# Sharing out the norm's last steps otherwise, and the next input's affine on ScalarE alone

## The chip, the cores and the metric

The kernel runs on one core of one Trainium2 chip. The metric is the device time of one execution in microseconds; less is better. The profile is of one execution by the hardware profiler, with its own time.

## The reference, cut to what matters

A two-layer network on 256 context and 512 latent tokens of width 1024. Each layer has an FFN, a mixer (a gated recurrence with pooling in layer 0, differential attention in layer 1) and a second FFN; a layer norm follows each of them, and the next sub-step's input is the norm's output scaled and shifted, with other factors for context and for latent tokens.

```python
def modulate(x, shift, scale):
    return x * (1.0 + scale) + shift

def ffn_substep(x, mods, w_in, w_out, g, b):
    shift, scale, gate = mods
    y = swiglu(modulate(x, shift, scale), w_in, w_out)
    return layer_norm(ALPHA * x + MACARON * gate * y, g, b)
...
x = ffn_substep(x, m_lat[0:3], ...)
ctx = ffn_substep(ctx, m_ctx[0:3], ...)
h_lat = modulate(x, m_lat[3], m_lat[4])
h_ctx = modulate(ctx, m_ctx[3], m_ctx[4])
```

## The kernel before, in words

**Layout.** Features lie on the 128 partitions, in KB = 8 blocks of 128; tokens lie along the row, context (0 to 256) first, then latent (256 to 768). Products are made in three passes for accuracy: each operand is split into a rounded high part and a remainder. `split` (lines 117 to 119) casts the high part on ScalarE and subtracts on VectorE (or GpSimd) for the low part. `mm3` (lines 157 to 159) issues high x high, high x low and low x high.

**An output product** is `out_phase`. It has two passes over the same weights, for two spans of tokens, the halves: for three FFNs and the even mixer tokens 0 to 512 and 512 to 768 (`FULL`), for the odd mixer and the last FFN 256 to 512 and 512 to 768 (`LATS`). A pass has nh steps kk, each over 256 rows of the weights: 11 for an FFN, 4 for a mixer. A step is two groups q of 24 matmuls. `operands` splits a step's g tile and its two weight tiles; in an FFN's second pass the weights' high and low parts go to tiles named `spare`, of which there are 11, shared with the first half's data. `fetch` starts the loads two steps ahead on SyncE's queue, into the four buffers of `raw`.

**The norm of the first half** runs during the second pass. `layer_norm` is a generator with 22 yields: four for sums, one for the mean, eight for the deviations and their squares, one for the variance and its inverse root rs, and eight final steps j, one for each feature block. After each step of the second pass `out_phase` takes three of them (-(-25 // 11) for an FFN) or seven (for a mixer). A final step j multiplies `r` by rs on VectorE (line 329), makes the next input `h` from it segment by segment (the first segment on ScalarE, line 336, the second on GpSimd, line 338), splits `h` into `xh` and `xl` (ScalarE, VectorE), makes the residual in place in `r` on GpSimd (line 344), and writes that to `ax` in memory on SyncE's queue (line 348). In the last FFN there is no next input: the final step makes the output in place, on ScalarE or GpSimd by turns, and writes it. The norm of the second half has only latent tokens; it goes on under the next sub-step's first products.

**Order.** The framework's planner fixes each engine's instruction order when the kernel is built, from readiness in a timing model of its own and, among ready ones, from the order in the program; buffers limit how far it runs ahead. On the chip each engine goes through its queue in order.

Of the kernel before, what the change touches and what calls it, by code (L numbers as in the profile page):

```python
# [15 lines left out]
AF = mybir.ActivationFunctionType  # L16
ALU = mybir.AluOpType
# [25 lines left out]
class Net:  # L43
# [255 lines left out]
    def layer_norm(self, half, halves, aff, nxt, ax_new, r_of, s1, done, table):  # L299
        nc = self.nc  # L300
        c0, c1 = halves[half]
        n = c1 - c0
        for j in range(done, KB):
            self.add_up(s1, r_of(half, j), j)
            if j % 2:
                yield
        pm = self.mean(s1, n, half)
        s2 = self.sums(n)
        yield
        for j in range(KB):  # L310
            r = r_of(half, j)
            nc.vector.tensor_sub(out=r, in0=r, in1=pm)
            sq = s2[j] if j < 2 else self.tmp("sq")[:, :n]
            i = nc.scalar.activation(out=sq, in_=r, func=AF.Square)
            if j == 0 and not half:
                self.table(LOGEXP, i)
            if j > 1:
                self.add_up(s2, sq, j)
            yield
        pv = self.mean(s2, n, half)  # L320
        rs, rt = self.tmp("rs"), self.tmp("rt")
        i = self.rsqrt(pv, self.eps_ln, LN_EPS, rs[:, :n], rt[:, :n])
        if half and table:
            self.settled = i
            self.table(table, i)
        yield
        for j in range(KB):
            r = r_of(half, j)
            nc.vector.tensor_mul(out=r, in0=r, in1=rs[:, :n])
            if nxt is not None:  # L330
                h = self.tmp("h")
                for x, (v, a, b) in enumerate(self.segs(c0, c1)):
                    o, i, sc, sh = h[:, a - c0:b - c0], r[:, a - c0:b - c0], aff[:, 2 + 2 * v, j:j + 1], \
                        aff[:, 3 + 2 * v, j:j + 1]
                    if x == 0:
                        nc.scalar.activation(out=o, in_=i, func=AF.Identity, scale=sc, bias=sh)
                    else:
                        nc.gpsimd.tensor_scalar(out=o, in0=i, scalar1=sc, scalar2=sh, op0=ALU.mult, op1=ALU.add)
                self.split(self.xh[:, j, c0:c1], self.xl[:, j, c0:c1], h[:, :n])
            g, b = aff[:, 0, j:j + 1], aff[:, 1, j:j + 1]  # L340
            if nxt is None and j % 2:
                nc.scalar.activation(out=r, in_=r, func=AF.Identity, scale=g, bias=b)
            else:
                nc.gpsimd.tensor_scalar(out=r, in0=r, scalar1=g, scalar2=b, op0=ALU.mult, op1=ALU.add)
            if nxt is None:
                nc.sync.dma_start(out=self.out[:, j, c0 - NCTX:c1 - NCTX], in_=r)
            else:
                nc.sync.dma_start(out=ax_new[:, j, c0:c1], in_=r)
            yield
# [18 lines left out]
    def out_phase(self, pool, nk, wsrc, gload, halves, gate, l, i, nxt, r_of, table=None, keep=False, ada=iter(())):  # L368


        nc = self.nc
        aff = self.affine(l, i, nxt)
# [4 lines left out]
        nh = nk // 2  # L377
        steps = [(p, kk) for p in range(2) for kk in range(nh)]

        kept, loaded, held = {}, {}, []  # L380

        def fetch(step):

            half, kk = step
            if half:
                loaded[step] = [gload(kk, *halves[half])]
                if not keep:
                    loaded[step] += [self.raw() for q in range(2)]
                for q, r in enumerate(loaded[step][1:]):
                    nc.sync.dma_start(out=r, in_=wsrc(q, kk))  # L390

        def operands(step):
            half, kk = step
            g, *raw = loaded.pop(step, (None,))
            g = self.pair2(gload(kk, *halves[half]) if g is None else g, halves[half][1] - halves[half][0])
            if raw:
                ws = []
                for r in raw:
                    ws.append([self.spare(pool, F32R) for _ in range(2)])
                    self.split(*ws[-1], r)  # L400
                return g, ws
            if not half:
                ws = [self.weights(wsrc(q, kk), "vector", pool if keep and kk else None) for q in range(2)]
                if not keep:
                    return g, ws
                kept[kk] = ws
            return g, kept[kk]
# [3 lines left out]
        for n_step, (half, kk) in enumerate(steps):  # L411
            c0, c1 = halves[half]
            n = c1 - c0
            if kk == 0:
                if n > 256:
                    out = [self.ps("st" if f == KB - 1 else "h")[:, :n] for f in range(KB)]
                else:
                    two = [self.ps() for f in range(KB // 2)]
                    out = [two[f // 2][:, f % 2 * n:f % 2 * n + n] for f in range(KB)]

            def products(kk, ops, q):
                (gh, gl), ws = ops
                wh, wl = ws[q]
                for k2 in range(2):
                    for f in range(4):
                        w0 = k2 * 512 + f * P
                        self.mm3(out[4 * q + f], wh[:, w0:w0 + P], wl[:, w0:w0 + P], gh[:, k2, :], gl[:, k2, :],
                                 kk + k2 == 0 and (n > 256 or f % 2 == 0),
                                 2 * kk + k2 == nk - 1 and (n > 256 or f % 2 == 1))

            if nxt is None and half and kk >= nh - 2:
                held.append((kk, ops))
                if kk == nh - 1:
                    for _ in norm:
                        pass
                    self.finale(held, products, out, gate, aff, [r_of(1, j) for j in range(KB)], halves[1])
                    break
            else:
                for q in range(2):
                    products(kk, ops, q)  # L440
            if n_step + 1 < len(steps):
                ops = operands(steps[n_step + 1])
            if n_step + 2 < len(steps):
                fetch(steps[n_step + 2])
            if half == 0:
                with self.behind_weights():
                    next(ada, None)
            if kk == 1:
                if half:
                    self.RB = self.late().rearrange("p (k c) -> p k c", k=KB)  # L450
                for j in range(KB):
                    self.residual(r_of(half, j), j, c0, c1)
            if half:
                for _ in range(-(-25 // nh)):
                    next(norm, None)
            if kk < nh - 1:
                continue
            if half:
                for _ in norm:
                    pass  # L460
            s1 = self.sums(n)
            for j in range(KB):
                r = r_of(half, j)
                for (v, a, b) in self.segs(c0, c1):
                    nc.vector.scalar_tensor_tensor(
                        out=r[:, a - c0:b - c0], in0=out[j][:, a - c0:b - c0],
                        scalar=self.col(*gate, v, j), in1=r[:, a - c0:b - c0], op0=ALU.mult, op1=ALU.add)
                if half:
                    self.add_up(s1, r, j)
            norm = self.layer_norm(half, halves, aff, nxt, ax_new, r_of, s1, KB if half else 0, table)  # L470
# [989 lines left out]
```

## Time and profile before

| | us |
|---|---|
| median of 3 runs | 2761.28 |
| lowest, highest | 2757.34, 2761.32 |
| the profiled execution's own time | 2760.27 |
| its span, first to last instruction | 2758.1 |

The mean granted TensorE clock of the profiled execution is 0.99 of full speed. PE is TensorE, PEld its weight loads, DVE VectorE, ACT ScalarE, POOL GpSimd, SP SyncE; a q behind the name is the engine's queue of DMA issues. L119 is line 119 of the kernel before. In the views an instruction is named by what it writes and reads, as `xh<-h`, with partitions x elements. What an engine waited for stands behind its idle time as `<-` and the engine, tile and line that ended it. A full clock is 1.00, half of it 0.50.

### The profile page before, as it was taken

The numbers are of one execution on the slowest core, as the hardware profiler recorded it, in microseconds if no ns is written. First come the engines' busy times: TensorE is split into PE (matmuls) and PEld (weight loads), VectorE is DVE, ScalarE is ACT, GpSimd is POOL, SyncE is SP. The second block draws the span as 40 slices with busy tenths as digits, with TensorE's granted clock in tenths as the row PEclk, the third lists the DMA queues.
The fourth block names the chain that finished last, engine by engine and source line by source line (L and its number), as shares of the span: only waits on it lengthen the run. The fifth ranks groups of instructions, "written<-read, shape, count | busy, mean of one in ns | idle before, by whom it ended". The sixth has DMA issues, their size and how long they took to land. (4 is left out here: it accounts for less than half of the span.)

```text
span 2758.1 us, 43943 instructions
## 1 busy us (share of the span) xinstructions
PE 2667.8 (97%) x17386; PEld 2435.0 (88%) x17386; DVE 1966.3 (71%) x2922; ACT 1221.4 (44%) x1922; POOL 888.1 (32%) x680
## 2 busy tenths in 40 slices
PE   8999999999989999999999999999999998999998
PEld 6999988987778789999888999988887777999997
DVE  4899677847764789977786776556827786787666
ACT  3433433634442533433254444423534655555554
POOL 2545300422110554440055444201422211465302
PEclk9999999999999999999999999999999999999999
DMA  6443266521104334426663432265521112433563
GB/s 250 138 155 129 88 244 231 202 78 68 45 22 168 111 131 143 140 91 221 217 201 117 172 123 78 94 230 197 199 77 47 35 39 79 140 100 116 171 212 129
DMA packets 138770, 374.20 MB, mean 136 GB/s; under 512 B 16066, under 2 KB 47170, under 8 KB 138564
## 3 DMA queue, kind: packets, MB, share of 16 engines
q1 hardware_dynamic: 136256, 369.68, 38.6%
q8 instruction: 136, 2.23, 0.3%
q10 hardware_dynamic: 2308, 1.72, 0.2%
q14 instruction: 70, 0.57, 0.1%
HBM read 337.78 MB, written 33.56 MB: 135 GB/s over the span
## 5 line engine op out<-in xcount | busy, mean ns | idle before, releaser
L117 ACT CAST r4h<-raw 128x1024 fp32r<-128x1024 f32 (+1 forms) x322 | 332.8, 1035 | 625.7 <-PE ps L158 325.0
L157 PE MATMUL ps<-xh,r4h 128*128 128x512 f32 (+2 forms) x1732 | 583.7, 339 | 11.4 <-ACT xh L117 7.6
L158 PE MATMUL ps<-xl,r4h 128*128 128x512 f32 (+2 forms) x1732 | 580.8, 336 | 0.5 <-DVE xl L119 0.4
L159 PE MATMUL ps<-xh,r4l 128*128 128x512 f32 (+2 forms) x1732 | 580.4, 336 | 0.4 <-DVE r4l L119 0.4
L119 DVE TENSOR_TENSOR r4l<-raw,r4h 128x1024 fp32r<-128x1024 f32 (+1 forms) x306 | 373.2, 1221 | 223.5 <-ACT r4h L117 163.6
L157 PEld LDWEIGHTS ps<-xh,r4h 128*128 128x128 f32 x1732 | 326.5, 189 | 41.3 <-ACT xh L117 10.1
L158 PEld LDWEIGHTS ps<-xl,r4h 128*128 128x128 f32 x1732 | 327.4, 189 | 22.9 <-DVE xl L119 2.0
L159 PEld LDWEIGHTS ps<-xh,r4l 128*128 128x128 f32 x1732 | 327.8, 189 | 22.2 <-DVE r4l L119 0.9
L157 PE MATMUL ps<-six,r4h 128*128 128x384 f32 (+1 forms) x852 | 278.3, 327 | 6.0 <-ACT c L788 6.0
L157 PE MATMUL ps<-r4h 128*128 128x512 f32 (+1 forms) x768 | 276.4, 360 | 1.1 <-DVE g L903 1.1
L159 PE MATMUL ps<-r4h,r4l 128*128 128x512 f32 (+1 forms) x768 | 275.3, 359 | 0.7 <-DVE r4l L119 0.7
L158 PE MATMUL ps<-six,r4h 128*128 128x384 f32 (+1 forms) x852 | 275.9, 324 | 0.0
L159 PE MATMUL ps<-six,r4l 128*128 128x384 f32 (+1 forms) x852 | 275.4, 323 | 0.0
L158 PE MATMUL ps<-r4l,r4h 128*128 128x512 f32 (+1 forms) x768 | 275.3, 359 | 0.0
L159 PE MATMUL ps<-r4h,spare 128*128 128x256 f32 (+1 forms) x896 | 262.4, 293 | 9.8 <-DVE spare L119 9.8
L157 PE MATMUL ps<-r4h,spare 128*128 128x256 f32 (+1 forms) x896 | 266.0, 297 | 4.0 <-ACT spare L117 4.0
L158 PE MATMUL ps<-r4l,spare 128*128 128x256 f32 (+1 forms) x896 | 261.4, 292 | 0.0
L760 POOL TENSOR_TENSOR raw<-raw,late 128x512 f32<-128x512 f32 x71 | 93.6, 1319 | 400.4 <-DVE r4l L119 388.5
L119 DVE TENSOR_TENSOR r4l<-late,r4h 128x1024 fp32r<-128x1024 f32 x71 | 106.1, 1495 | 115.1 <-PE ps L158 97.2
L159 PEld LDWEIGHTS ps<-r4h,spare 128*128 128x128 f32 x896 | 174.8, 195 | 13.2 <-DVE spare L119 11.3
L157 PEld LDWEIGHTS ps<-r4h,spare 128*128 128x128 f32 x896 | 175.0, 195 | 8.6 <-ACT spare L117 4.6
L185 DVE SCALAR_TENSOR_TENSOR trash<-spare 128x1024 bf16<-128x1024 f32 x112 | 181.1, 1618 | 1.0 <-DMA spare<-in_w_ada 0.9
(313 smaller groups left out, 5646.6 us busy)
## 6 DMA issues: line engine op xcount, KB each, us to landing
raw<-in_w_ffn_in SPq DMA_DIRECT2D x176, 512.0 KB, 3.5
raw<-in_w_ffn_out SPq DMA_DIRECT2D x176, 512.0 KB, 4.3
spare<-in_w_ada SPq DMA_DIRECT2D x80, 512.0 KB, 5.3
six<-in_w_ada SPq DMA_DIRECT2D x64, 512.0 KB, 5.7
g<-late_g SPq DMA_DIRECT2D x88, 128.0 KB, 2.1
six<-g SPq DMA_DIRECT2D x44, 256.0 KB, 3.7
raw<-in_w_in_even SPq DMA_DIRECT2D x20, 512.0 KB, 3.5
raw<-in_w_in_odd SPq DMA_DIRECT2D x16, 512.0 KB, 3.4
```

The costliest lines, as they stand in the source:

```text
L117: self.copied = self.nc.scalar.copy(out=h, in_=src)
L119: eng.tensor_sub(out=l, in0=src, in1=h.bitcast(F32))
L157: mm(out=ps, lhsT=h, rhs=xh, start=first, stop=False)
L158: mm(out=ps, lhsT=h, rhs=xl, start=False, stop=False)
L159: mm(out=ps, lhsT=l, rhs=xh, start=False, stop=last)
L185: nc.vector.scalar_tensor_tensor(out=self.tmp("trash").bitcast(BF16), in0=r, scalar=1.0, in1=self.c_bc[v], op0=ALU.mult, op1=ALU.mult, acc ...
L760: nc.gpsimd.tensor_sub(out=a12, in0=a12, in1=sums[:, 512:])
```

## The change

It does two things. In a final step, all segments of `h` are made on ScalarE, where the second was on GpSimd. And where nh is 11, the steps of the norm that follow kk = 0 to 10 are given by a list, 3, 3, 3, 3, 3, 2, 2, 2, 2, 1, 1, where it was three after each; elsewhere the number stays. The computation is the same.

```diff
             if nxt is not None:
                 h = self.tmp("h")
-                for x, (v, a, b) in enumerate(self.segs(c0, c1)):
-                    o, i, sc, sh = h[:, a - c0:b - c0], r[:, a - c0:b - c0], aff[:, 2 + 2 * v, j:j + 1], \
-                        aff[:, 3 + 2 * v, j:j + 1]
-                    if x == 0:
-                        nc.scalar.activation(out=o, in_=i, func=AF.Identity, scale=sc, bias=sh)
-                    else:
-                        nc.gpsimd.tensor_scalar(out=o, in0=i, scalar1=sc, scalar2=sh, op0=ALU.mult, op1=ALU.add)
+                for v, a, b in self.segs(c0, c1):
+                    nc.scalar.activation(out=h[:, a - c0:b - c0], in_=r[:, a - c0:b - c0], func=AF.Identity,
+                                         scale=aff[:, 2 + 2 * v, j:j + 1], bias=aff[:, 3 + 2 * v, j:j + 1])
                 self.split(self.xh[:, j, c0:c1], self.xl[:, j, c0:c1], h[:, :n])
...
         kept, loaded, held = {}, {}, []
+
+
+        steps_of = (3, 3, 3, 3, 3, 2, 2, 2, 2, 1, 1) if nh == 11 else [-(-25 // nh)] * nh
...
             if half:
-                for _ in range(-(-25 // nh)):
+                for _ in range(steps_of[kk]):
                     next(norm, None)
```

## Rows read from the trace of the kernel before

**Rows 1.** The page's first part: busy time, share and instructions of each engine.

```profile
PE 2667.8 (97%) x17386; PEld 2435.0 (88%) x17386; DVE 1966.3 (71%) x2922; ACT 1221.4 (44%) x1922; POOL 888.1 (32%) x680
```

**Rows 2.** TensorE's waits over the whole run: total us, times, longest.

```profile
PE ps L159 <- DVE spare L119: 9.8, 7, 1.9
...
PE ps L157 <- ACT spare L117: 4.0, 3, 1.3
```

**Rows 3.** TensorE's timeline, first FFN's output product: start, duration, idle before.

```profile
532.11 0.39 PE L159 MATMUL ps<-r4h,spare 128*128 128x256 f32 x1 [1.16 <-DVE spare L119]
532.34 0.28 PE L157 MATMUL ps<-r4h,spare 128*128 128x256 f32 x1
532.46 0.28 PE L158 MATMUL ps<-r4l,spare 128*128 128x256 f32 x1
...
536.34 0.39 PE L157 MATMUL ps<-r4h,spare 128*128 128x256 f32 x1 [1.33 <-ACT spare L117]
...
538.79 0.58 PE L159 MATMUL ps<-r4h,spare 128*128 128x256 f32 x1 [1.94 <-DVE spare L119]
...
540.02 0.41 PE L158 MATMUL ps<-r4l,spare 128*128 128x256 f32 x1
540.24 0.42 PE L159 MATMUL ps<-r4h,spare 128*128 128x256 f32 x1
```

**Rows 4.** Stages: length, busy us (instructions) by engine, PEclk, DMA share, GB/s.

```profile
518.00:546.00 28.00, 23.57 (x172) 22.96 (x172) 22.02 (x27) 15.97 (x24) 21.66 (x16) 0.88 0.50 174
536.00:546.00 10.00, 7.71 (x42) 7.51 (x43) 9.05 (x10) 5.83 (x8) 5.50 (x3) 0.66 0.73 249
1444.00:1454.00 10.00, 8.06 (x45) 7.85 (x45) 8.58 (x9) 5.29 (x8) 4.88 (x3) 0.66 0.79 263
1972.00:1982.00 10.00, 7.77 (x51) 7.56 (x52) 9.05 (x10) 5.85 (x8) 5.46 (x3) 0.83 0.77 253
922.00:928.00 6.00, 5.14 (x16) 3.78 (x15) 4.34 (x6) 2.79 (x6) 6.00 (x7) 0.72 0.25 96
```

The engines stand in the order PE, PEld, DVE, ACT, POOL.

**Rows 5.** ScalarE's timeline in the same stage as rows 3.

```profile
527.37 1.04 ACT L117 CAST spare<-raw 128x1024 fp32r<-128x1024 f32 x1
529.34 0.60 ACT L336 ACTIVATE h<-spare,aff 128x256 f32<-128x256 f32 x1 [0.93 <-DVE spare L329]
532.36 0.62 ACT L117 CAST xh<-h 128x512 fp32r<-128x512 f32 x1 [2.41 <-POOL h L338]
532.88 1.09 ACT L336 ACTIVATE h<-spare,aff 128x256 f32<-128x256 f32 x2
...
535.25 1.99 ACT L117 CAST spare<-raw 128x1024 fp32r<-128x1024 f32 x2
```

**Rows 6.** Groups by line from 518 to 546: busy us, mean ns | idle before, releaser.

```profile
L119 DVE TENSOR_TENSOR xl<-h,xh 128x512 fp32r<-128x512 f32 x8 | 6.3, 805 | 5.9 <-ACT xh L117 5.9
...
L117 ACT CAST xh<-h 128x512 fp32r<-128x512 f32 x8 | 4.8, 620 | 8.3 <-POOL h L338 8.3
...
L119 DVE TENSOR_TENSOR r4l<-six,r4h 128x512 fp32r<-128x512 f32 x2 | 1.4, 679 | 0.0
```

**Rows 7.** Line 338 (GpSimd's affine), whole run: ns minimum/median/maximum, first and last start.

```profile
L338 POOL TENSOR_SCALAR h<-six,aff x12: 548/1260/2035, 519.7 to 1962.2; 128x256 f32<-128x256 f32 x12
L338 POOL TENSOR_SCALAR h<-spare,aff x12: 551/1768/3088, 529.8 to 1973.6; 128x256 f32<-128x256 f32 x12
L338 POOL TENSOR_SCALAR h<-R,aff x8: 547/767/2022, 918.1 to 934.0; 128x256 f32<-128x256 f32 x8
```

**Rows 8.** VectorE's timeline in the last FFN's output product.

```profile
2718.28 1.23 DVE L119 TENSOR_TENSOR spare<-raw,spare 128x1024 fp32r<-128x1024 f32 x1 [0.64 <-DMA out<-spare]
...
2733.89 1.66 DVE L485 SCALAR_TENSOR_TENSOR late<-ps,mod,late 128x256 f32<-128x256 f32 x4 [6.76 <-PE ps L159]
```

**Rows 9.** TensorE's waits from 878 to 962, the even mixer's output and after it.

```profile
PE ps L157 <- ACT xh L117: 3.5, 3, 1.6
```

**Rows 10.** VectorE's timeline after the even mixer's output product.

```profile
933.37 1.26 DVE L465 SCALAR_TENSOR_TENSOR late<-ps,mod,late 128x256 f32<-128x256 f32 x3
```

## The prediction

> **What bounds the kernel now.** I read the page's first part, then TensorE's waits, then the stages in which those waits lie, engine by engine. TensorE is busy 2667.8 of 2758.1 us [rows 1], so another engine counts only where it makes TensorE wait or lets its clock fall. Two of its waits belong to `out_phase`: those for `spare`, the split weights of the output product's second pass, 9.8 us at line 159 and 4.0 at line 157 [rows 2].
>
> In the first FFN's output product they are three gaps within 8 us: 1.16, 1.33 and 1.94, together 4.43 us [rows 3]. The first and the third wait for VectorE's low part of a weight tile, the second for ScalarE's high part. They have a tail: after the first gap matmuls still start 0.12 us apart, after the third 0.22 [rows 3]. The granted clock says the same: its mean is 0.66 of full speed in the ten microseconds from 536 and from 1444, and 0.83 from 1972 [rows 4], that is 1.2 instead of 2.4 GHz for 6.8, 6.8 and 3.4 us.
>
> Why the weight tiles are late is read on ScalarE [rows 5]. Its `xh` casts wait for GpSimd's part of `h` (2.41 us in the row, 8.3 us in the eight casts of one FFN [rows 6]), and the casts of the weights stand behind them in the same queue: the pair that ends the second gap starts at 535.25, right after two `xh` casts. GpSimd's 128x256 affine takes 547 to 551 ns at best, but 1260 and 1768 at the median in the FFNs and up to 3088 [rows 7]: it is slow beside VectorE, which is busy 22.02 of the 28 us from 518 to 546 [rows 4] and waits another 5.9 for `xh` [rows 6]. VectorE is never idle otherwise, and so the next in line.
>
> **The change, part by part.** Three FFNs have this stage with two segments (tokens 0 to 512: 256 context and 256 latent); the even mixer's output has it too. The odd mixer and the last FFN have one segment in it, which ScalarE makes already.
>
> *Affine moved.* GpSimd loses 12 + 12 + 8 = 32 instructions [rows 7], eight per stage, and ScalarE gains them. Two of ScalarE's in a row take 1.09 us, a cast of `xh` 0.62 [rows 5]: 1.71 us a step, 13.7 for eight. Before, a step was 0.55 + 0.62 us and the wait: 8 x 1.17 + 8.3 = 17.7 us. ScalarE's queue is therefore through the steps 4 us sooner, though it works 8 x 0.55 = 4.4 us more. The residual's affine (L344) stays on GpSimd; it rewrites `r`, so it now waits for two ScalarE instructions where one of the two readers was on its own queue. Behind it stands SyncE's write of `ax`, and behind that, in SyncE's queue, the load of weights two steps on. No write is added, and this chain too loses the slow GpSimd affine, so I cost it at nothing; if its cover, the two steps by which loads run ahead, were gone, the load itself would be the next thing late.
>
> *Steps shared out.* The norm has 22 yields. Up to kk = 4 both lists hand out 15 steps; then 3, 3, 1 become 2, 2, 2, 1, so three of the last steps come one slot later, each with its affine, cast, subtraction and `ax` write. A slot is 48 matmuls at 0.12 us, 5.8 us. ScalarE's need in a slot is 0.62 us for g, 1.99 for two weight tiles [rows 5] and 3.42 for two steps: 6.0 us; with three steps 7.7. VectorE's is 2 x 1.23 [rows 8] + 0.68 for weights and g and 2 x (0.68 + 0.68) [rows 6] for the steps: 5.9 us. With two steps a slot both engines about keep pace, and the slots by which weights run ahead of TensorE cover the rest. Whether the queues follow the list I can't show: the planner orders by readiness, and all eight steps become ready together, when their common factor rs is there.
>
> *What it is worth in the FFNs.* At stake are three times 4.43 = 13.3 us of gaps, and the slow clock: of its 17 us some 14.3 are matmuls (the rest lies in the gap before them), which at 0.12 instead of 0.215 us would save 44%: 6.3 us. Together 19.6. The bounds: all of it, or nothing, if VectorE takes ScalarE's place. For VectorE, 22.0 us of work stand against the 28 - 4.4 - 2.1 = 21.5 us that the stage would last, so it must give back some of what GpSimd costs it. Its subtractions for `xl` average 805 ns where the same shape for g takes 679 [rows 6]: 8 x 0.13 = 1.0 us, of which half may go with half of GpSimd's instructions. That leaves 21.5 in 21.5, with the lead of the weights to even it out. I keep 1 us of gap per FFN, alone too short to slow the clock, as the first gap shows [rows 3]: 19.6 - 3.0 = 16.6 us.
>
> The Trainium skill, in "SBUF — State Buffer", section "SBUF: two separate sides", says that a GpSimd instruction and a VectorE one with two SBUF inputs shut each other out for the whole of the instruction. By it each instruction removed would give VectorE its 0.55 us back, 4.4 per FFN, and the sum would be the full 19.6. The trace bears that out for GpSimd, whose 0.55 us grow to 3.09, and hardly for VectorE, so I stay with the rows.
>
> *The even mixer.* There `xh` is used at once: TensorE waits 3.5 us for it [rows 9], at a clock of 0.72 in the six microseconds from 922 [rows 4]. That is 3.4 us at half speed, 1.5 lost: about 5 at stake. But the second half's norm stands behind these steps on VectorE, where its residual additions (L465) go on at 933.37 [rows 10], and TensorE wants that half next. The gain is bounded by what the steps bring this forward; between 0 and 5 I take the middle, 2.5.
>
> *The last FFN.* Its three steps come a slot later. A subtraction of weights at 2718.28 waits for their `out` write [rows 8]. The tile that it fills is for the held products of kk = 9. These and those of kk = 10, in their first parts, 5.8 us, end where L485 goes on at 2733.89 [rows 8], so they begin at 2728.1. From 2719.5, when the tile is there, 8.6 us cover a delay of at most 5.8: nothing. With that cover gone, each microsecond beyond it would be one at the end.
>
> **Sum.** The profiled execution took 2760.27 us, 2.2 more than its span and 1.0 below the median of the runs, 2761.28. 2760.3 - 16.6 - 2.5 = 2741.2.
>
> **Rivals.** *VectorE is next.* Two of the gaps wait for VectorE. If multiplications and subtractions of the steps still hold the low parts back, only ScalarE's gap goes and half of the slow stretch, 1.33 + 1.05 = 2.4 us per FFN: 2753; if half of VectorE's gaps go as well (1.55), 2748. For it: 22.02 us busy. Against: its 5.9 us of waits are for `xh`, and end with the change.
>
> *Nothing changes.* The list does nothing since readiness rules, and the planner leaves the weight casts behind the same steps, so that ScalarE's own 4.4 us of new work, and its wait for VectorE's multiplication, stand where the waits stood: 2756 to 2764.
>
> *Slower: ScalarE becomes the bound.* If the planner puts all eight steps ahead of the weight cast that starts at 527.37 [rows 5], and they don't overlap (0.60 + 0.60 + 0.62 = 1.82 us), that cast starts 14.6 us after the first step at 519.7 [rows 7], at 534.3. It and the subtraction take 1.05 + 1.23 us, so the low part is there at 536.6, where TensorE wants it at 530.9 (the first gap's end less its 1.16). One gap of 5.7 us and a slow stretch of the longer kind, 44% of 6 us = 2.6, make 8.3 per FFN, against 4.43 + 2.1 = 6.5 now: 5.4 us in all, 2766. It decides from a cast later than 532.5, where gap and stretch are level with now. Against it: before, that cast went ahead of the steps that were listed right after it, and the list now puts fewer ahead.
>
> **How the numbers follow.** The forecast has 0.63: the wait it removes is in the rows three times over, and only the queues' new order is unknown. VectorE next has 0.21, nothing 0.11, slower 0.05. The forecast's own range is 2736 (all of 19.6, and 4.7 in the mixer) to 2748. To hold 8 in 10 the range goes on through the VectorE case: 2736 to 2756. A measurement of this kernel tells about 0.2%, 5.5 us, from no change. Faster is the forecast and nearly all of the VectorE case, 0.83; same 0.12; slower 0.05.
>
> **What would show it.** Right: GpSimd at 648 instructions instead of 680 and ScalarE at 32 more than its 1922 [rows 1]; TensorE's waits for `spare` under 4 us instead of 13.8; a granted clock of 1.00 in the three FFN stages; no wait of the `xh` casts for GpSimd. Wrong: the waits for `spare` at line 159 stay above 6 us with VectorE busy throughout (VectorE next); weight casts late behind ScalarE's own steps (slower); new waits outside these stages, because the planner's order moved there too.

## The result and the profile after

The changed kernel took 2733.89 us (median of 4 runs, 2730.01 to 2740.74) against 2759.31 for the kernel before, run beside it (4 runs): a ratio of 0.9911, 95% interval 0.9888 to 0.9934. Forecast were 2741.2, with 2736 to 2756. It is faster, as forecast, and by more than the range allowed: 2.1 us below its lower end. In two later measurements the same kernel had medians of 2736.87 and 2735.59, with ratios of 0.9921 (0.9909 to 0.9934) and 0.9912 (0.9895 to 0.9928): one just inside the range, one 0.4 us outside.

The page's first part after, beside [rows 1]: GpSimd has 32 instructions fewer and ScalarE 32 more, as counted.

```profile
PE 2653.1 (97%) x17386; PEld 2420.8 (89%) x17386; DVE 1963.3 (72%) x2922; ACT 1233.4 (45%) x1954; POOL 874.7 (32%) x648
```

TensorE's waits after, over the whole run, answer to [rows 2]: total us, times, longest. (The wait for `xh` was 7.6 us over the whole run before.)

```profile
PE ps L157 <- ACT xh L117: 3.8, 3, 2.5
...
PE ps L1325 <- DVE late L464: 2.9, 1, 2.9
...
PE ps L159 <- DVE spare L119: 0.8, 1, 0.8
```

Of the 13.8 us of waits for `spare`, 0.8 are left, and these lie in the odd mixer's output; line 157 no longer waits for ScalarE's `spare` at all. The row between is a new wait, for `late` at line 1325, which is the odd mixer's first product. Lines after 338 are lower by 4 in the changed kernel.

The three second passes of the FFN output products, each from its first matmul to its last, show the main gain. First before, then after: window, length, busy us (instructions) of PE, PEld, DVE, ACT, POOL, then PEclk, DMA share, GB/s.

```profile
482.80:555.40 72.60, 68.17 (x533) 66.60 (x532) 59.22 (x80) 41.90 (x58) 35.24 (x25) 0.95 0.60 204
1390.20:1463.00 72.80, 68.35 (x533) 66.78 (x532) 58.81 (x79) 41.65 (x57) 34.75 (x25) 0.95 0.61 205
1918.70:1990.30 71.60, 67.16 (x533) 65.56 (x532) 56.95 (x72) 41.81 (x57) 30.48 (x23) 0.98 0.58 195
```

```profile
483.00:548.00 65.00, 65.00 (x533) 64.00 (x533) 56.65 (x74) 44.31 (x66) 31.10 (x14) 1.00 0.62 210
1378.30:1443.30 65.00, 65.00 (x533) 64.02 (x532) 55.72 (x72) 44.87 (x65) 30.15 (x14) 1.00 0.62 214
1900.20:1965.20 65.00, 65.00 (x534) 64.00 (x533) 53.86 (x68) 43.90 (x64) 26.61 (x13) 1.00 0.58 197
```

TensorE is busy in all 65.00 us of each pass, and the clock is 1.00. The three took 217.0 us and take 195.0: 22.0 us are gone here (22.1 from the first matmul's start to the last's), and there is no wait left in them to remove.

How it came about is read on ScalarE and VectorE, in the stretch of [rows 5]. ScalarE's timeline after (start, duration):

```profile
526.53 0.60 ACT L333 ACTIVATE h<-spare,aff 128x256 f32<-128x256 f32 x1
527.04 1.03 ACT L117 CAST spare<-raw 128x1024 fp32r<-128x1024 f32 x1
527.98 0.61 ACT L117 CAST xh<-h 128x512 fp32r<-128x512 f32 x1
528.50 1.04 ACT L117 CAST spare<-raw 128x1024 fp32r<-128x1024 f32 x1
```

VectorE's timeline after, around the low part that ends the first gap in [rows 3]:

```profile
529.44 1.21 DVE L119 TENSOR_TENSOR spare<-raw,spare 128x1024 fp32r<-128x1024 f32 x1
530.57 1.09 DVE L119 TENSOR_TENSOR xl<-h,xh 128x512 fp32r<-128x512 f32 x1
```

No row has a wait in brackets. ScalarE goes from affine to cast to affine, and the weight casts stand between the steps. The low part is there at 529.44 + 1.21 = 530.65, and the matmul of line 159 that reads it starts on time at 531.07: 0.4 us to spare (the expectations below say 0.3).

### The profile page after: what moved, and what is told of

Same layout as the page of the kernel before. It is cut to its first block, busy times and chain, and to the rows that moved or that the text cites. A ratio compares the mean times of both kernels' runs of the same rounds, so it can differ in the third digit from the quotient of the medians.

```text
span 2731.8 us, 43932 instructions
## 1 busy us (share of the span) xinstructions
PE 2653.1 (97%) x17386; PEld 2420.8 (89%) x17386; DVE 1963.3 (72%) x2922; ACT 1233.4 (45%) x1954; POOL 874.7 (32%) x648
## 5 line engine op out<-in xcount | busy, mean ns | idle before, releaser
L157 PE MATMUL ps<-r4h,spare 128*128 128x256 f32 (+1 forms) x896 | 262.7, 293 | 0.1
L159 PE MATMUL ps<-r4h,spare 128*128 128x256 f32 (+1 forms) x896 | 258.5, 289 | 0.8 <-DVE spare L119 0.8
L157 PEld LDWEIGHTS ps<-r4h,spare 128*128 128x128 f32 x896 | 171.7, 192 | 4.3 <-issue 1.9
L158 PEld LDWEIGHTS ps<-r4l,spare 128*128 128x128 f32 x896 | 171.7, 192 | 4.0 <-issue 1.9
```

What stands on the lines that cost most here:

```text
L157: mm(out=ps, lhsT=h, rhs=xh, start=first, stop=False)
L158: mm(out=ps, lhsT=h, rhs=xl, start=False, stop=False)
L159: mm(out=ps, lhsT=l, rhs=xh, start=False, stop=last)
```

## The experiments

All are made from the changed kernel, and each ratio is to the kernel before, run beside it. In the table, "FFN passes" is the sum of the three second passes, from first matmul to last; "mixer" runs from the even mixer's second output pass to the end of the next FFN's input product; "odd" is the odd mixer's input product, "att." the last stretch of its attention.

| kernel | median us | ratio, 95% | FFN passes | mixer | odd | att. |
|---|---|---|---|---|---|---|
| before | 2758 to 2760 | 1 | 216.9 | 377.6 | 91.5 | 43.2 |
| changed | 2733.89 | 0.9911 (0.9888 to 0.9934) | 194.8 | 371.2 | 94.7 | 39.9 |
| changed, second time | 2736.87 | 0.9921 (0.9909 to 0.9934) | 194.8 | 375.0 | 93.2 | 43.0 |
| changed, third time | 2735.59 | 0.9912 (0.9895 to 0.9928) | 194.9 | 373.5 | 95.1 | 43.1 |
| affine alone | 2742.42 | 0.9946 (0.9931 to 0.9961) | 205.5 | 372.1 | 92.1 | 41.4 |
| list alone | 2747.55 | 0.9963 (0.9949 to 0.9977) | 201.7 | 377.7 | 93.0 | 39.9 |
| affine on VectorE | 2743.77 | 0.9945 (0.993 to 0.996) | 197.1 | 377.3 | 93.4 | 41.2 |
| mixer's affine on GpSimd | 2741.41 | 0.9941 (0.9926 to 0.9956) | 194.8 | 378.2 | 93.7 | 43.1 |
| writes of ax from GpSimd | 2751.99 | 0.9977 (0.9967 to 0.9988) | 202.6 | 379.4 | 91.8 | 43.1 |
| half of residuals on ScalarE | 2731.18 | 0.9901 (0.9885 to 0.9916) | 195.5 | 373.8 | 91.5 | 39.9 |
| the same again | 2732.48 | 0.9901 (0.9886 to 0.9916) | 194.8 | 370.6 | 91.5 | 41.4 |
| all residuals on ScalarE | 2737.9 | 0.9923 (0.9907 to 0.994) | 200.0 | 374.0 | 91.5 | 41.4 |

The stretches, in us, are of one profiled execution each, the medians of 4 to 11.

**The affine alone.** The list is taken back.

```diff
-        steps_of = (3, 3, 3, 3, 3, 2, 2, 2, 2, 1, 1) if nh == 11 else [-(-25 // nh)] * nh
+        steps_of = [-(-25 // nh)] * nh
```

> Only the affine is moved to ScalarE; the steps are handed out three at a time as before. Theory A (GpSimd in ScalarE's way was the cause): most of the gain stays. In the planner's order the weight tile that TensorE wants at about 531 us now stands behind two more final steps on ScalarE and VectorE (some 3 us), so one gap of 1 to 2.5 us comes back in each of the three FFNs, with or without a slow stretch: 2738 to 2747 us against 2734 for both parts. Theory B (the list did it): 2750 us or more. The even mixer is as fast as with both parts in either theory.

Measured 2742.42, in theory A's range, but only part of it at the place that it named. The wait of ScalarE for GpSimd is gone, yet each pass keeps some 2 us of gaps, four of them. In the first pass the first two, 0.15 and 0.52 us, lie where theory A had them: ScalarE's casts start 47.0 and 48.4 us after the pass's first matmul instead of 44.0 and 45.4, behind two more steps. The larger two come 12 us later; here is TensorE's timeline (idle before in brackets), and behind it ScalarE's cast and SyncE's issues in the same stretch:

```profile
545.86 0.39 PE L157 MATMUL ps<-r4h,spare 128*128 128x256 f32 x1 [0.52 <-ACT spare L117]
...
547.17 0.38 PE L159 MATMUL ps<-r4h,spare 128*128 128x256 f32 x1 [0.81 <-DVE spare L119]
```

```profile
544.76 1.04 ACT L117 CAST spare<-raw 128x1024 fp32r<-128x1024 f32 x1 [6.62 <-DMA raw<-in_w_ffn_out]
```

```profile
534.50 5.85 SPq L344 DMA_DIRECT2D ax<-spare  x3
540.44 0.89 SPq L389 DMA_DIRECT2D raw<-in_w_ffn_out  x2
```

The last two loads of weights stand behind three writes of `ax`, each of which waits for GpSimd's residual affine. SyncE's timeline of the changed kernel, with the list, has one write ahead of them:

```profile
533.91 0.32 SPq L344 DMA_DIRECT2D ax<-spare  x1
534.33 0.88 SPq L389 DMA_DIRECT2D raw<-in_w_ffn_out  x2
```

The pass itself begins at 484.71 here and at 483.06 with the list, so the loads go out 55.7 and 51.3 us into it: 4.5 us earlier with the list. Of the first pass's 2.0 us of gaps 1.3 come by SyncE's queue and 0.7 by ScalarE's: in this stage the list does more in SyncE's queue than in those of the engines that compute, on which the prediction had costed it.

**The list alone.** The second segment goes back to GpSimd.

```diff
-                    nc.scalar.activation(out=h[:, a - c0:b - c0], in_=r[:, a - c0:b - c0], func=AF.Identity,
...
+                    if x == 0:
+                        nc.scalar.activation(out=o, in_=i, func=AF.Identity, scale=sc, bias=sh)
+                    else:
+                        nc.gpsimd.tensor_scalar(out=o, in0=i, scalar1=sc, scalar2=sh, op0=ALU.mult, op1=ALU.add)
```

> Only the list is changed; the second segment's affine stays on GpSimd. Theory A: ScalarE still waits some 8 us per FFN for GpSimd, but in two slots one step fewer stands ahead of a weight cast, so between a tenth and a half of the FFNs' 22 us goes: 2748 to 2758 us, with gaps still there for the spare tiles and a granted clock under 0.9 in the ten microseconds after. Theory B: 2735 to 2742. The even mixer keeps its waits for xh (3.5 us) in both.

Measured 2747.55, half a microsecond under the edge of theory A and far from theory B. ScalarE's groups from 518 to 551 show that the wait for GpSimd is there as before (8.3 us in [rows 6]):

```profile
L117 ACT CAST xh<-h 128x512 fp32r<-128x512 f32 x8 | 4.8, 621 | 7.6 <-POOL h L338 7.6
```

It costs less: the first pass keeps 2.2 us of gaps instead of 4.4, at a clock of 1.00. ScalarE's timeline shows casts of weights earlier between those that wait:

```profile
524.68 1.03 ACT L117 CAST spare<-raw 128x1024 fp32r<-128x1024 f32 x1
...
531.55 2.00 ACT L117 CAST spare<-raw 128x1024 fp32r<-128x1024 f32 x2
```

The pass begins at 483.63 here and at 482.79 in the kernel before, so these casts start 41.1 and 47.9 us into it, where those of 527.37 and 535.25 in [rows 5] started at 44.6 and 52.5. In the passes the affine alone is worth 11.4 us, the list alone 15.2, both 22.1: they share part of the gain. Theory A had allowed the list half of the 22 at most, with a granted clock under 0.9 behind the gaps, and was wrong in both; the mixer, at 377.7 us, keeps all of its loss, as expected.

**The affine on VectorE.** Both parts of the change are kept, but the second segment goes to VectorE.

```diff
-                    nc.scalar.activation(out=h[:, a - c0:b - c0], in_=r[:, a - c0:b - c0], func=AF.Identity,
...
+                    if x == 0:
+                        nc.scalar.activation(out=o, in_=i, func=AF.Identity, scale=sc, bias=sh)
+                    else:
+                        nc.vector.tensor_scalar(out=o, in0=i, scalar1=sc, scalar2=sh, op0=ALU.mult, op1=ALU.add)
```

> Both parts, but the second segment's affine on VectorE instead of ScalarE. A 128x256 affine should take VectorE about 0.29 us (the 128x256 scale-and-add of the inverse root takes that), 2.3 us per FFN for eight. If VectorE is the engine with nothing left (its low part is ready about 0.3 us before TensorE wants it with both parts), gaps of 1 to 2.5 us come back in each FFN: 2738 to 2748. If instead ScalarE is the tighter one, it is relieved of 4 us per FFN and the time is 2734 or less.

Measured 2743.77, in the middle of what was expected, but not by the road expected. VectorE's groups from 518 to 546, and the first pass by windows:

```profile
L338 DVE TENSOR_SCALAR h<-spare,aff 128x256 f32<-128x256 f32 x4 | 2.3, 592 | 0.0
L338 DVE TENSOR_SCALAR h<-six,aff 128x256 f32<-128x256 f32 x4 | 1.9, 484 | 0.0
```

```profile
484.20:550.00 65.80, 65.27 (x533) 64.09 (x532) 58.96 (x81) 40.79 (x57) 33.72 (x14) 1.00 0.64 208
```

VectorE has 2.3 + 1.9 = 4.2 us more to do in the stage, and TensorE loses 0.53 us in gaps and 0.8 in all. So VectorE was not at its limit: much of what it has to do there (the eight `xl`) is wanted only when the pass is over, and the low parts of the weights stand between these in its queue. About half of what this kernel loses against the changed one is lost in the mixer, 377.3 us as if nothing had been changed there; 2.3 us are lost in the passes and 2.5 in the input of the FFN ahead of the odd mixer.

**The mixer's affine on GpSimd.** ScalarE makes all of it in the FFNs only.

```diff
-                    nc.scalar.activation(out=h[:, a - c0:b - c0], in_=r[:, a - c0:b - c0], func=AF.Identity,
...
+                    if x == 0 or not self.in_mixer:
+                        nc.scalar.activation(out=o, in_=i, func=AF.Identity, scale=sc, bias=sh)
+                    else:
+                        nc.gpsimd.tensor_scalar(out=o, in0=i, scalar1=sc, scalar2=sh, op0=ALU.mult, op1=ALU.add)
...
+        self.in_mixer = nk == 8
```

> Both parts in the FFNs, but in the even mixer's output the second segment stays on GpSimd. If the mixer's share is what the two traces show between its second pass and the next FFN's output product (6.4 us), the time is 2740 us and TensorE's waits for xh there are 3.5 us again with a slow clock behind them; if that share belongs to something else in the planner's order, it is 2734.

Measured 2741.41, against 2733.89 to 2736.87 for the changed kernel at other times; the FFN passes are the same and the mixer's stretch is that of before. TensorE's waits from 885 to 1263 in this kernel, then from 887 to 1258 in the changed one:

```profile
PE ps L157 <- ACT xh L117: 3.5, 3, 1.6
```

```profile
PE ps L157 <- ACT xh L117: 0.3, 1, 0.3
```

The mixer's share is therefore shown apart from the rest. Its size: three kernels whose mixer's second segment is not on ScalarE (list alone, VectorE, this one) take 377.3 to 378.2 us for the stretch, the changed kernel 371.2, 375.0 and 373.5, so 2.6 to 6.4 and in the mean 4.4 us of gain against 377.6 before. The expectation's 6.4 was the largest of these.

**The changed kernel again.**

> The changed kernel once more, unedited, for the spread of one and the same program. The three second passes of the FFN output products are fixed by 528 matmuls at 0.12 us and should read 64.9 us each at a clock of 1.00 again, the stretch after the even mixer's output about 344 us. The attention stage, which read 39.8 us at a granted clock of 1.00 in the changed kernel and 43.1 at 0.91 in the one before with the same 11.1 us of gaps, may read either if its clock is a matter of when the gaps fall; if the change itself mended it, it reads 39.8 again. Median 2730 to 2740, against some 2758 before.

The passes repeat to 0.1 us. The attention stage does not: by windows, before, then the changed kernel's first and second profile:

```profile
2284.00:2327.20 43.20, 32.10 (x223) 25.90 (x223) 28.16 (x43) 25.94 (x47) 7.01 (x9) 0.91 0.12 43
```

```profile
2262.10:2302.00 39.90, 28.82 (x224) 23.22 (x223) 28.08 (x43) 25.93 (x47) 7.00 (x9) 1.00 0.12 43
```

```profile
2262.80:2305.80 43.00, 31.88 (x224) 25.73 (x223) 28.12 (x43) 25.96 (x47) 7.04 (x9) 0.90 0.12 43
```

One program, the same 11.1 us of gaps in its matmuls, and the clock is 1.00 in one execution and 0.90 in another. The 3.3 us that the first profile showed as won in this stage are not the change's; over the twelve profiles in the table the stage reads 39.9 three times, 41.2 to 41.4 four times and 43.0 to 43.2 five times, whatever the kernel.

**Writes of `ax` from GpSimd's queue.** This and the next three ask about the new wait of 2.93 us ahead of the odd mixer. In the changed kernel's timeline, TensorE, then GpSimd and SyncE:

```profile
1970.51 0.50 PE L1325 MATMUL ps<-r4h,xh 128*128 128x512 f32 x1 [2.93 <-DVE late L464]
```

```profile
1938.41 9.93 POOL L340 TENSOR_SCALAR six<-six,aff 128x512 f32<-128x512 f32 x4 [10.87 <-DVE six L329]
1948.33 8.50 POOL L340 TENSOR_SCALAR spare<-spare,aff 128x512 f32<-128x512 f32 x4
```

```profile
1954.41 2.02 SPq L344 DMA_DIRECT2D ax<-spare  x2
1956.52 0.88 SPq L124 DMA_DIRECT2D raw<-in_w_v_odd  x2
```

SyncE issues the first load of the odd mixer's V weights at 1956.52, 8.8 us before the mixer's first matmul at 1965.3. In the kernel before, SyncE's timeline has all eight from 1978.00 on, 12.4 us before 1990.4:

```profile
1978.00 17.52 SPq L124 DMA_DIRECT2D raw<-in_w_v_odd  x8
```

The load is not later in itself. From the first matmul of the pass (1918.7 before, 1900.2 after) it goes out after 59.3 us before and 56.3 after. But TensorE is through the pass in 65.0 us instead of 71.6, so that 3.6 us of its lead are gone. SyncE's waits for GpSimd in the same stage of the kernel before, 18.9 us in all, were no shorter than the 16.7 after:

```profile
SPq L348 <- POOL six L344: 9.8, 4, 6.3
SPq L348 <- POOL spare L344: 9.1, 4, 3.0
```

VectorE's timeline after shows how a late load becomes a wait of TensorE: the split of the late weight stands in the queue ahead of the residual that is wanted.

```profile
1968.44 1.22 DVE L119 TENSOR_TENSOR r4l<-raw,r4h 128x1024 fp32r<-128x1024 f32 x1 [2.08 <-ACT r4h L117]
1969.58 1.65 DVE L464 SCALAR_TENSOR_TENSOR late<-ps,mod,late 128x256 f32<-128x256 f32 x4
```


```diff
-                nc.sync.dma_start(out=ax_new[:, j, c0:c1], in_=r)
+                (nc.sync if half else nc.gpsimd).dma_start(out=ax_new[:, j, c0:c1], in_=r)
```

> Edit: the writes of ax for the first half go to GpSimd's own DMA queue, right behind the affine that they wait for, and leave SyncE's queue; the order on TensorE, VectorE and ScalarE is the same instruction for instruction. Theory A (SyncE's queue holds up the next weights): in the changed kernel SyncE waits 16.7 us for GpSimd's residual affine in this stage and issues the first load of the odd mixer's V weights 8.8 us before TensorE is through, against 12.4 before, and TensorE then waits 2.93 us. Without the writes in its queue the load is issued at least 11 us ahead, the wait falls below 0.5 us and the median 2 to 4 us below that of the unedited kernel of the same call. Rival B (the transfers set the pace, the DMA engines being 99% busy there): the wait stays between 2 and 3.5 us and the median within 1.5 us. Rival C (issuing from GpSimd costs its affines or the traffic more than it frees): the median rises by over 2 us.

The wait is gone (the odd mixer's input takes 91.8 us), as theory A said, and the whole is 15 us slower than the changed kernel measured beside it, as rival C said. GpSimd's timeline and VectorE's show the price:

```profile
539.75 0.77 POOL L340 TENSOR_SCALAR spare<-spare,aff 128x512 f32<-128x512 f32 x1
540.81 0.59 POOL L344 DMA_DIRECT2D ax<-spare  x1 [0.30 <-POOL spare L340]
```

```profile
545.06 2.36 DVE L119 TENSOR_TENSOR spare<-raw,spare 128x1024 fp32r<-128x1024 f32 x2 [5.71 <-DMA ax<-spare]
```

Each write costs GpSimd 0.3 + 0.6 us, which its next affine waits out. And the writes hold up something else: the last low parts of the weights go into the very buffers from which `ax` is written, so VectorE now waits 5.71 us for a write to land, and TensorE 2.9 for VectorE. The passes lose 7.8 us by this; the mixer's stretch loses 4.4, and the way from the odd mixer's output to the last FFN's 5.8, which were not traced further.

**Half of the residuals on ScalarE.** GpSimd makes four of the eight per stage.

```diff
-            if nxt is None and j % 2:
+            if j % 2 and (nxt is None or not half):
```

> Edit: the residual's affine of the first half goes to ScalarE for odd blocks, four of eight per stage, 4 x 0.61 = 2.4 us more on ScalarE in each FFN stage and four instructions of 2.1 to 2.5 us fewer on GpSimd. Theory A (SyncE's queue, as above): GpSimd is through some 8 us earlier, the ax writes with it, and the odd mixer's wait of 2.93 falls below 1 us; nothing is lost in the FFN stages if ScalarE has the room; median 1 to 4 us below the unedited kernel of the same call. Rival (ScalarE becomes the bound, the slower case of the prediction): the low parts of the weights are ready 0.3 us ahead of TensorE at their tightest, so 2.4 us more in ScalarE's queue brings gaps back in the second passes, 0.5 to 2 us in each, and the median rises by 2 to 8 us.

Measured 2731.18 against 2736.87 for the changed kernel beside it: theory A, and a little more. The instruction took longer than expected, 812 ns instead of 610 (ScalarE's group, whole run):

```profile
L338 ACT ACTIVATE six<-six,aff 128x512 f32<-128x512 f32 x6 | 4.9, 812 | 0.0
```

so 3.2 us more per stage, which ScalarE had to give: the passes are at 194.8 to 195.5. SyncE's waits from 1935 to 1972, first in the changed kernel, then in this one:

```profile
SPq L344 <- POOL six L340: 11.1, 4, 5.4
...
SPq L344 <- POOL spare L340: 5.6, 3, 2.4
```

```profile
SPq L344 <- POOL six L340: 6.9, 2, 5.4
...
SPq L344 <- POOL spare L340: 2.3, 2, 1.3
```

The wait for GpSimd falls from 16.7 us to 9.2, with 2.4 for ScalarE; the first load goes out 11.7 us ahead of the odd mixer instead of 8.8, and the mixer's input has no wait. The advantage was near the spread of one program, so both kernels were measured once more, side by side:

> The kernel with the residual affine of odd blocks on ScalarE once more, beside the unedited changed kernel in the same call, since its 5.7 us of advantage are near the spread of one program between executions (the attention stage alone reads 39.8 or 42.9 us in the same kernel). If the advantage is the shorter chain through GpSimd and SyncE, the input of the FFN after the mixer's second FFN stage and of the odd mixer read 335.8 and 91.5 us again, without a wait for the residual, some 2.5 to 4 us less than the unedited kernel, and the median is 2 to 6 us lower. If it was the spread, the medians agree within 1.5 us.

> The changed kernel, unedited, as the other side of that comparison: median 2733 to 2738, the odd mixer's input with a wait for the residual of 1.4 to 3 us, the three second passes of the FFN output products at 64.9 us each; the attention stage at either 39.8 or 42.9 us.

2732.48 against 2735.59. The odd mixer's input reads 91.5 us again, 3.6 less than in the changed kernel beside it, and the FFN's input ahead of it 335.9 against 337.1. The medians differ by 5.7 and 3.1 us. This version is the fastest of those tried.

**All of them on ScalarE.**

```diff
-            if nxt is None and j % 2:
+            if (nxt is None and j % 2) or (nxt is not None and not half):
```

> Edit: all eight residual affines of the first half of each norm go from GpSimd to ScalarE, 8 x 0.61 = 4.9 us more on ScalarE in each FFN stage, where the run with four of them on ScalarE added 2.4 and had one gap of 0.44 us in three second passes. Theory A (ScalarE has no more room: the slower case of the prediction, now with its price): its casts of weights come late and the second passes show gaps of 1 to 3 us each, so that the median lies 3 to 12 us above the 2731 of the run with four. Rival (the wait for GpSimd was what counted, ScalarE's casts of weights stay ahead): no gaps over 0.5 us, the median between 2727 and 2733, and no wait of SyncE for GpSimd in these stages.

Measured 2737.9, 6.7 us above the kernel with four, some 5 of them in the passes: ScalarE has no more room. The gaps are smaller than expected, 0.83 us in the first pass by windows, but they come in every pass:

```profile
485.90:552.50 66.60, 65.77 (x533) 64.19 (x532) 55.99 (x78) 50.55 (x74) 14.52 (x9) 1.00 0.64 209
```

VectorE's timeline shows the low part that ends the first of them waiting for ScalarE's cast:

```profile
533.75 1.22 DVE L119 TENSOR_TENSOR spare<-raw,spare 128x1024 fp32r<-128x1024 f32 x1 [1.46 <-ACT spare L117]
```

The mechanism of the prediction's slower rival exists, then, though at this price the kernel is still 20 us faster than the one before. It takes 8 x 0.81 = 6.5 us of ScalarE's time on top of the change, and half of that is nearly free.

## Why the prediction was right or wrong

**What bounds the kernel: right.** The waits for `spare`, the slow clock behind them and the wait of `xh` for GpSimd went together, and with them 22.1 us in the three passes. Taking the second segment back to GpSimd brings back the wait of 7.6 us and 5.0 of the 13.3 us of gaps. That is less than half: with the wait still there the list alone gains 15.2 us in the passes, so the place of the weights' casts in ScalarE's queue counted at least as much as the wait ahead of them. How the gain would divide between its two parts the prediction had not said. It has four, not three, of the last steps come a slot later (3, 3, 1 against 2, 2, 2, 1); no term of its sum hangs on that.

**The stake in the FFNs: too small, 19.6 for 22.1.** The gaps (13.3) and the slow clock were priced well. The latter can be counted from matmul to matmul in the kernel before: 63 starts in the three passes are 0.213 us behind the one before instead of 0.12, which makes 5.9, and the three first ones at the slow clock, at 0.38, another 0.5: 6.4 against 6.3. What was missing is the price of a gap beside its length. Behind the gap of 1.16 us in [rows 3] the next matmul starts not 0.12 but 0.23 us later, and from the start before the gap to the start after it are 1.44 us, not 1.16 + 0.12. That makes some 0.27 us for each of nine gaps, 2.4 in all: 13.3 + 6.4 + 2.4 = 22.1. The prediction put this term at nothing, and took 19.6 as the most that could be won; the range's lower end of 2736 was built on it. The kernel with the affine alone confirms it: its first pass is 3.0 us longer than 64.9 for 2.0 us of gaps at a clock of 1.00, with four gaps.

**1 us of gap kept back per FFN: wrong, the largest of the errors.** The step was "That leaves 21.5 in 21.5, with the lead of the weights to even it out. I keep 1 us of gap per FFN". The balance was about right: after the change VectorE has no wait from 518 to 538.3, and is busy for 20.79 of the 22 us to 540:

```profile
518.00:540.00 22.00, 22.00 (x186) 22.00 (x185) 20.79 (x27) 18.46 (x32) 18.42 (x8) 1.00 0.50 178
```

The conclusion was not: it gave all of that work one deadline, and only the low parts of the weights have it. With 4.2 us more on VectorE (and about as much less on ScalarE) the pass grew by 0.8 us. 16.6 forecast, 22.1 measured: 3.0 for what was kept back and 2.5 for the gaps' own price.

**The even mixer: right in kind, 2.5 for 4.4** (2.6 to 6.4), inside its bounds of 0 to 5 but for one execution. The middle was taken because the second half's residuals stand behind the steps on VectorE. They came forward as well: in [rows 10] they went on at 933.4 and the last pair started at 937.5; after the change, in a pass that begins 5.8 us sooner, the last pair starts at 924.7, 7.0 us earlier in the stage.

**SyncE's queue at nothing: wrong.** The step was "this chain too loses the slow GpSimd affine, so I cost it at nothing". It lost that instruction, but the other one, the residual's, grew to twice its length. By groups over the whole run, before and after:

```profile
L344 POOL TENSOR_SCALAR six<-six,aff 128x512 f32<-128x512 f32 x12 | 15.1, 1263 | 0.0
L344 POOL TENSOR_SCALAR spare<-spare,aff 128x512 f32<-128x512 f32 x12 | 13.6, 1133 | 0.6
```

```profile
L340 POOL TENSOR_SCALAR six<-six,aff 128x512 f32<-128x512 f32 x12 | 29.8, 2493 | 31.7 <-DVE six L329 31.7
L340 POOL TENSOR_SCALAR spare<-spare,aff 128x512 f32<-128x512 f32 x12 | 25.5, 2138 | 0.0
```

So the chain as a whole did not grow, but it lost less than TensorE: in the stage ahead of the odd mixer GpSimd took 21.9 us from its first to its last instruction before (1955.68 to 1977.56) and takes 18.4 after, and the next stage's load goes out 3.0 us sooner in its pass. TensorE's pass lost 6.6. What the step left out is that the gain in the passes eats the lead of the load, unless the chain shortens by as much. The sentence named what would be late next, a load of weights, and that is what came, one stage on: 1.7 to 3.6 us in the odd mixer's input and 1.2 in the FFN input before it. (The wait for `late` was 2.9, 1.5 and 1.8 us in the changed kernel's three profiles; in the third a clock of 0.98 in this stretch goes with the rest.) Half of the residuals on ScalarE gives these back. The lead alone does not set the wait: all residuals on ScalarE leave 10.9 us of it and no wait, the list alone 11.0 and 1.5 us.

**The last FFN at nothing: right** (its output product took 129.2 us and takes 128.3).

**VectorE next, nothing changes: neither came.** The list does reach the queues, SyncE's above all. Sum of the errors: 5.5 in the passes and 1.9 in the mixer too little, some 4 in the odd mixer and the input before it too much, which hides half of the first two. The forecast's gain was 19.1 us on the profiled execution, 22.5 with these; measured were 25.4, 22.0 and 24.5 in the three measurements. In the profile of the first the attention stage's 3.3 us come on top, and those are luck.

**What GpSimd costs VectorE.** VectorE's subtractions for `xl` took 805 ns on average before, 782 after the change and 686 without any GpSimd affine in the stage (all residuals on ScalarE). In the timeline of the changed kernel single ones stand at 1.09 us among others of 0.68, 0.41 more; six of VectorE's instructions in the first pass are longer by that, 2.4 us in all. GpSimd's own instruction of 0.77 us when VectorE is idle takes 2.1 to 2.5: 18.4 us for eight instead of 6.2. Most of the loss is on GpSimd's side, as the prediction had read it from the rows. By the Trainium skill, "SBUF — State Buffer", section "SBUF: two separate sides", each GpSimd instruction gone should give VectorE its whole length back; worked out from that, as an estimate, the eight would cost VectorE 8 x 0.77 = 6.2 us. The measured 2.4 decide.

## What to carry to other kernels

A stage that is made shorter takes lead away from whatever was loaded under it: follow the chains that run beside it into the DMA queue, where writes stand ahead of the next stage's loads, and price how much sooner they end than the stage does. A slow engine's remaining instructions may also grow when its neighbour no longer waits. A gap costs its length, a restart, and in some executions a stretch at half clock; count all three from start to start. When an engine looks full, give each piece of its work its own deadline before pricing it as the bound.

## What was not expected of the hardware

The same stage of the same program, with the same 11.1 us of gaps in its matmuls, ran at a granted clock of 1.00 in one execution and 0.90 in another, 3.1 us apart. In one execution of the kernel with the affine alone, gaps of 2.0, 2.2 and 1.9 us in all left the clock of an FFN pass at 1.00 in the first and the third, and were followed by 3.4 us at 0.5 in the second; with the list alone 2.2 us left it at 1.00 twice. What decides between these was not tried.

GpSimd's 128x512 affine takes 0.77 us beside an idle VectorE and 2.1 to 2.5 beside a busy one.
